# One encoder layer on one core: the residual rebuilt by TensorE, layer-norm scale and shift moved to evictions, first feed-forward pair's weight combinations kept

## The chip, the cores and the metric

The kernel runs on one core of a Trainium2 chip. The number that counts is the device time of one execution in microseconds (us), the median of several. The core's engines are PE (matrix multiply; PEld is its weight load), DVE (vector), ACT (scalar and activations), POOL (the third elementwise engine) and SP, which issues most of the DMA transfers. Each engine works through its own queue in order, so an instruction that waits holds up everything queued behind it on that engine.

## The reference

One layer, S = 1024 positions, D = 1024 channels, float32 in and out:

```
h = LN(x; ln0)
p = h @ w_in                        # 1024 -> 2048
y = [S5(p), RWKV-7(h, p), conv(p), Fourier(p)]
h = LN(alpha * h + y @ w_out; ln1)  # alpha = 2 ** 0.25
f = (silu(h @ w1) * (h @ w3)) @ w2  # 1024 -> 2816 -> 1024
out = LN(alpha * h + f; ln2)
```

LN subtracts the row mean, multiplies by the reciprocal deviation, then by a gain g and adds a shift b per channel. RWKV-7 is a scan over positions in two directions.

## The kernel before

Float32 products are made of three: each operand is split into a high part, cast to the type fp32r, and the low remainder, and `mm3` (L160 to L162) adds hi·hi, hi·lo and lo·hi in PSUM. `split_to` makes the parts: an ACT cast (L1384), then a subtraction on DVE or POOL (L1385).

**Order of the work.** `Trunk.build` weaves two generators with a list scheduler that sets each engine's queue order: `chain()` at high priority (S5, then the RWKV scan) and `beside()` (input projections, convolution, Fourier part, the second direction's preparation, output weights). The normalized input h lies transposed (channels on partitions) as `hhi` and `hlo` in the tiles HA0, HA1, HB0, HB1 until the last input projection; then these tiles take the data of the scan's other direction (HA0f to HB1f), which "inverse" and then the scan read.

**Output projection** (L1412 to L1500). For each tile t of 128 rows, from 7 down to 0: `residual` loads x and makes alpha·h again in row layout (L1432 DVE, L1434 POOL, L1435 DVE; the rows alpha·g, alpha·b, ln1_g, ln1_b come from `out_first`); `out_load` loads y and splits it (the subtraction on DVE for tiles 7 and 6, without a fixed engine for the rest); `out_product` runs 48 matmuls and adds PSUM to the residual (L1455); `norm` takes statistics and makes two passes (L1465, L1466). For each pair of tiles `turn` transposes on PE (L1518), copies out of PSUM on ACT (L1519), multiplies by alpha (L1520), stores to `d_acc`, and forms seven sums and differences of blocks, H[0] (first 512 positions, turns 0 and 1) or H[1] (turns 2 and 3).

**Feed-forward.** Products are made by a seven-multiplication scheme on 2 x 2 blocks. `ff_hidden` goes over 11 pairs p; each needs seven combinations of w1 and seven of w3, made by `ff_stream` (L1554 to L1583) in rings of tiles. Pair 0 runs as two halves of positions, `(0, (0,))` and `(0, (1,))`, so its first half can start before turns 2 and 3; the combinations are loaded and made once for each half. `put_by` splits and stores results to `d_f`. `ff_second` multiplies by w2: seven products n of 11 pairs, results added into `acc`; at n == 3 each of the eight `d_acc` tiles is loaded and added (L1783).

## Time and profile before

| what | value |
|---|---|
| median of 3 runs | 1462.27 us (1462.12 to 1463.15) |
| the profiled execution, own time | 1465.01 us |
| its span, first to last instruction | 1462.2 us |
| mean granted TensorE clock in it | 0.958 of full speed |
| PE, DVE, ACT, POOL busy | 90%, 75%, 43%, 39% |
| input projections; last matmul | to 454.8 us |
| output projection; last matmul | to 772.9 us |
| second stage of the feed-forward | 1228.8 to 1451.9 us |

How to read the rows below. A row of busy time gives the stretch, its length, then busy us of PE, PEld, DVE, ACT and POOL, each with its count of instructions in parentheses, then the granted TensorE clock, the DMA share and GB/s; "sum" adds all the tens of the query, also those not shown. A group of instructions has line, engine, operation, out<-in, shape and count, then busy us and mean ns of one, then the engine's idle time before it and what ended it. A wait has the total in us, how often, and the longest in us. A row on a tile's instructions has minimum, median and maximum ns, then the first and the last start.

### The profile page before, as it was taken

The numbers are of one execution on the slowest core, as the hardware profiler recorded it, in microseconds if no ns is written. First come the engines' busy times: TensorE is split into PE (matmuls) and PEld (weight loads), VectorE is DVE, ScalarE is ACT, GpSimd is POOL, SyncE is SP. The second block draws the span as 40 slices with busy tenths as digits, with TensorE's granted clock in tenths as the row PEclk, the third lists the DMA queues.
The fourth block names the chain that finished last, engine by engine and source line by source line (L and its number), as shares of the span: only waits on it lengthen the run. The fifth ranks groups of instructions, "written<-read, shape, count | busy, mean of one in ns | idle before, by whom it ended". The sixth has DMA issues, their size and how long they took to land.

```text
span 1462.2 us, 23749 instructions
## 1 busy us (share of the span) xinstructions
PE 1323.2 (90%) x9072; PEld 1196.4 (82%) x9072; DVE 1100.0 (75%) x1910; ACT 621.7 (43%) x1205; POOL 575.7 (39%) x524
## 2 busy tenths in 40 slices
PE   6968797977797999999877899999999999999997
...
GB/s 241 49 54 29 13 94 87 44 70 89 87 73 180 2 15 148 84 128 154 118 70 87 138 123 159 147 147 143 157 147 142 150 137 291 385 315 234 273 188 115
DMA packets 97056, 193.95 MB, mean 133 GB/s; under 512 B 24624, under 2 KB 50864, under 8 KB 96944
## 3 DMA queue, kind: packets, MB, share of 16 engines
...
## 4 chain that ended last, share of the span: by engine, by line
PE 42%; DVE 12%; DMA 3%; issue 2%; ACT 1%; POOL 1%; DVEq 0%; SPq 0%; ACTq 0%; POOLq 0%
PE fx L160 5%; PE fx L162 5%; PE fx L161 5%; PE f L160 4%; PE f L162 4%; PE f L161 4%; PE fy L162 2%; PE fy L160 2%; PE fy L161 2%; DVE acc L1435 1%; PE fz L160 1%; PE fz L161 1%; PE fz L162 1%; DMA fw<-w 1%; PE ops L161 1%
## 5 line engine op out<-in xcount | busy, mean ns | idle before, releaser
L160 PE MATMUL proj<-HA,wh 128*128 128x256 f32 x672 | 195.5, 291 | 14.6 <-DVE la L919 11.8
L160 PE MATMUL fx<-H,fc 128*128 128x256 f32 x704 | 196.9, 284 | 5.7 <-ACT fc L1384 2.2
L161 PE MATMUL proj<-HB,wh 128*128 128x256 f32 x672 | 200.1, 298 | 1.7 <-POOL HB L334 1.7
L162 PE MATMUL proj<-HA,wl 128*128 128x256 f32 x672 | 196.6, 293 | 4.1 <-POOL wl L394 4.1
L162 PE MATMUL fx<-H,fc 128*128 128x256 f32 x704 | 197.8, 282 | 2.6 <-DVE fc L1385 2.6
L1385 POOL TENSOR_TENSOR fc<-fw,fc 128x512 fp32r<-128x512 f32 x96 | 137.3, 1432 | 158.5 <-ACT fc L1384 157.7
L161 PE MATMUL fx<-H,fc 128*128 128x256 f32 x704 | 198.5, 282 | 0.0
L160 PEld LDWEIGHTS proj<-HA,wh 128*128 128x128 f32 x672 | 131.8, 196 | 18.4 <-issue 7.7
L162 PEld LDWEIGHTS proj<-HA,wl 128*128 128x128 f32 x672 | 131.5, 196 | 10.0 <-issue 5.5
L160 PEld LDWEIGHTS fx<-H,fc 128*128 128x128 f32 x704 | 132.5, 190 | 7.8 <-ACT fe L1633 2.7
L161 PEld LDWEIGHTS proj<-HB,wh 128*128 128x128 f32 x672 | 131.5, 196 | 7.0 <-issue 4.8
L162 PEld LDWEIGHTS fx<-H,fc 128*128 128x128 f32 x704 | 133.7, 191 | 2.8 <-DVE fc L1385 2.8
L161 PEld LDWEIGHTS fx<-H,fc 128*128 128x128 f32 x704 | 134.1, 191 | 0.1
L160 PE MATMUL f<-fb,fa 128*128 128x512 f32 x276 | 108.9, 395 | 0.0
L162 PE MATMUL f<-fb,fa 128*128 128x512 f32 x276 | 108.9, 394 | 0.0
L161 PE MATMUL f<-fb,fa 128*128 128x512 f32 x276 | 108.7, 394 | 0.0
L160 PE MATMUL fy<-H,fc 128*128 128x256 f32 x352 | 100.0, 284 | 4.7 <-ACT fe L1642 3.6
L162 PE MATMUL fy<-H,fc 128*128 128x256 f32 x352 | 99.5, 284 | 0.2 <-DVE fc L1385 0.2
L161 PE MATMUL fy<-H,fc 128*128 128x256 f32 x352 | 99.5, 283 | 0.0
L1821 POOL TENSOR_TENSOR acc<-acc,g 128x1024 f32<-128x1024 f32 x4 | 11.6, 2904 | 205.8 <-ACT acc L1820 205.8
L1384 ACT CAST fc<-fw 128x512 fp32r<-128x512 f32 x120 | 73.7, 619 | 31.8 <-POOL fc L1385 15.7
L1385 POOL TENSOR_TENSOR fc<-fs,fc 128x512 fp32r<-128x512 f32 x24 | 33.4, 1391 | 119.4 <-ACT fc L1384 116.0
...
## 6 DMA issues: line engine op xcount, KB each, us to landing
...
```

The source lines that it names most:

```text
L160: mm(out, whi, xhi, start=start, stop=False, skip_group_check=shared)
L161: mm(out, whi, xlo, start=False, stop=False, skip_group_check=shared)
L162: mm(out, wlo, xhi, start=False, stop=stop, skip_group_check=shared)
L1384: nc.scalar.copy(out=hi, in_=raw)
L1385: (eng or nc.gpsimd).tensor_tensor(out=lo, in0=raw, in1=hi.bitcast(F32), op=ALU.subtract)
L1435: nc.vector.tensor_tensor(out=ht, in0=ht, in1=self.row4[1], op=ALU.add)
L1821: nc.gpsimd.tensor_tensor(out=o, in0=o, in1=self.g2, op=ALU.mult)
```

## The change

1. `residuals()` turns h back to row layout on PE: 128 matmuls of 128x128 with `hhi` and `hlo` as stationary operand and an identity moving, in 16 groups of eight (one PSUM buffer of bank z), each group multiplied by alpha out of PSUM on ACT, and eight stores of 512 KB to `d_res`. It is woven with the convolution's projections. `residual` is now one load of `d_res`; its three passes, the four row loads and two ACT multiplications of `out_first` go.
2. `norm` is one DVE pass without g and b; `d_acc` is stored from there. `turn` applies g and b per channel while it leaves PSUM: four ACT activations of 128x128 in place of each copy of 128x512, and no multiplication by alpha. Turns 0 and 1 stand behind the output products of tiles 5 and 3.
3. `ff_second` makes up for it at n == 1 in place of n == 3: acc += alpha·b, x·(alpha·g) on POOL, acc += x.
4. In pair 0 the seven combinations of w1 are kept for both halves in a ring "k" (Z2, P2, P3, T7, WR, WH, WH); the order is w1 and w3 for half 0, then w1 and w3 for half 1, and results of pair 0 are put once at full width, 7 instead of 14.
5. `out_load` and `residual` of tile t - 1 are issued ahead of the product of tile t, and the split of y is always on DVE.

The diff, cut (the body of the loop in `ff_stream` moves into `parts` unchanged, and `ff_hidden` takes the steps of `ff_order`; `mm3` keeps its last matmul as `last_mm`, and `ff_second` loads the rows alpha·ln1_g and alpha·ln1_b first):

```diff
@@ -224,8 +225,10 @@
                     def beside():
-                        for part in (self.lora_project, self.rkv_project, self.conv, self.fourier_project):
+                        for part in (self.lora_project, self.rkv_project):
                             yield from part()
+                        yield from woven((self.conv(), 0), (self.residuals(), 0))
+                        yield from self.fourier_project()
...
@@ -268,6 +271,8 @@
+        self.ident_r = cp.tile([128, 128], R, name="ident_r")
+        nc.scalar.copy(out=self.ident_r, in_=self.ident)
@@ -1405,15 +1411,15 @@
+    def alpha_row(self, out, i):
+        self.row_load(out, i)
+        self.nc.scalar.mul(out=out, in_=out, mul=ALPHA)
-        rows = self.t("TT", [128, 4, D], "rows")
-        self.row4 = [rows[:, i] for i in range(4)]
-        for i in range(4):
-            self.row_load(rows[:, i], i)
-        for i in range(2):
-            nc.scalar.mul(out=rows[:, i], in_=rows[:, i], mul=ALPHA)
+        self.vec1 = self.cp.tile([128, 16], F32, name="vec1")
+        nc.scalar.dma_start(out=self.vec1, in_=self.A["vec1"])
@@ -1425,20 +1431,28 @@
         yield from self.out_product(7)
+    def residuals(self):
+        nc = self.nc
+        for t in range(NT - 1, -1, -1):
+            x = self.t(f"Z{t % 3}", [128, 2, 4, 128], "res")
+            for q in range(2):
+                ps = self.ps("z", [128, 4, 128], "rs")
+                for k in range(4):
+                    nc.tensor.matmul(ps[:, k, :], self.hhi[:, t, 4 * q + k, :], self.ident_r, start=True, stop=False)
+                    nc.tensor.matmul(ps[:, k, :], self.hlo[:, t, 4 * q + k, :], self.ident_r, start=False, stop=True)
+                nc.scalar.mul(out=x[:, q], in_=ps, mul=ALPHA)
+                yield 1.3
+            nc.sync.dma_start(out=self.d_res[t], in_=x.rearrange("p a k n -> p (a k n)"))
     def residual(self, t, tag):
-        nc = self.nc
-        ht = self.acc[t] = self.t(tag, [128, D], "acc")
-        nc.sync.dma_start(out=ht, in_=self.A["x"][t * 128:(t + 1) * 128, :])
-        nc.vector.tensor_scalar(out=ht, in0=ht, scalar1=self.st0[:, t, 0:1], scalar2=self.st0[:, t, 1:2],
-                                op0=ALU.subtract, op1=ALU.mult)
-        nc.gpsimd.tensor_tensor(out=ht, in0=ht, in1=self.row4[0], op=ALU.mult)
-        nc.vector.tensor_tensor(out=ht, in0=ht, in1=self.row4[1], op=ALU.add)
+        self.acc[t] = self.t(tag, [128, D], "acc")
+        self.nc.sync.dma_start(out=self.acc[t], in_=self.d_res[t])
     def out_load(self, t):
         nc = self.nc
         raw = self.raw("yraw").rearrange("p (k s) -> p k s", k=8)
         nc.sync.dma_start(out=raw, in_=self.d_y[:, :, t * 128:(t + 1) * 128].rearrange("k p s -> p k s"))
-        self.split_to(*self.y_parts(t), raw, nc.vector if t > 5 else None)
+        self.split_to(*self.y_parts(t), raw, nc.vector)
     def y_parts(self, t):
         return self.yp[t] if t < 7 else self.y7
@@ -1456,14 +1470,13 @@
     def out_proj(self):
         nc = self.nc
-        g1, b1 = self.row4[2:]
         self.raws = ["WR", "T7"]
         def norm(t):
             ht = self.acc[t]
             mean, rstd = self.row_stats(self.m, ht, D, LN_EPS)
-            nc.vector.scalar_tensor_tensor(out=ht, in0=ht, scalar=mean, in1=g1, op0=ALU.subtract, op1=ALU.mult)
-            nc.vector.scalar_tensor_tensor(out=ht, in0=ht, scalar=rstd, in1=b1, op0=ALU.mult, op1=ALU.add)
+            nc.vector.tensor_scalar(out=ht, in0=ht, scalar1=mean, scalar2=rstd, op0=ALU.subtract, op1=ALU.mult)
+            nc.sync.dma_start(out=self.d_acc[t], in_=ht)
         self.H = [[], []]
@@ -1478,14 +1491,16 @@
         self.out_load(6)
         self.residual(6, tag(6))
         for t in range(NT - 1, -1, -1):
-            if t < 7:
-                run(self.out_product(t))
             if 0 < t < 7:
                 self.out_load(t - 1)
                 self.residual(t - 1, tag(t - 1))
+            if t < 7:
+                run(self.out_product(t))
+            if t in (5, 3):
+                with self.tc.issue_after(self.last_mm.ins):
+                    self.turn(int(t == 3), [("P4", "P5", "Z0"), ("T6", "P0", "Z0")][t == 3])
             norm(t)
-            if t in (6, 4):
-                self.turn(3 - t // 2, [("P4", "P5", "Z0"), ("T6", "P0", "Z0")][t == 4])
             if t == 1:
                 self.combos = self.ff_stream()
                 self.ahead = [next(self.combos) for i in range(2)]
@@ -1516,9 +1531,11 @@
                 for k in range(4):
                     kt = 4 * q + k
                     nc.tensor.transpose(ps[:, k, :], ht[:, kt * 128:(kt + 1) * 128], self.ident)
-                nc.scalar.copy(out=dst[q], in_=ps)
-            nc.scalar.mul(out=ht, in_=ht, mul=ALPHA)
-            nc.sync.dma_start(out=self.d_acc[t], in_=ht)
+                for k in range(4):
+                    nc.scalar.activation(out=dst[q][:, k], in_=ps[:, k, :], func=AF.Identity,
+                                         scale=self.vec1[:, 4 * q + k:4 * q + k + 1],
+                                         bias=self.vec1[:, 8 + 4 * q + k:9 + 4 * q + k])
         H = self.H[j // 2]
         def put(i, x, eng):
@@ -1548,39 +1565,51 @@
     def ff_order(self):
-        return [(0, (0,)), (0, (1,))] + [(p, (0, 1)) for p in range(1, NF // 2)]
+        split = [(w, (h,)) for h in range(2) for w in range(2)]
+        return [split] + [[(w, (0, 1)) for w in range(2)] for p in range(1, NF // 2)]
     def ff_stream(self):
         nc, A = self.nc, self.A
         tt = nc.vector.tensor_tensor
-        self.rings = {"w": ["Z0", "Z1", "MW", "T6"], "s": ["P0", "P1"], "c": ["Z2", "P2", "LA0", "LA1", "C1", "C2"],
-                      "e": ["P3", "P4", "P5", "T5", "T7", "WR", "WL", "WL"], "g": ["WH", "WH"]}
+        self.rings = {"w": ["Z0", "Z1", "MW", "T6"], "s": ["P0", "P1"], "c": ["C1", "C2", "LA0", "LA1"],
+                      "e": ["P4", "P5", "T5", "WL", "WL"], "g": [], "k": ["Z2", "P2", "P3", "T7", "WR", "WH", "WH"]}
         self.banks = ["pj", "q", "fs", "q", "z", "pj", "q", "fs"]
         def split(x, eng=None):
-            c = self.ring("c", [128, 2, 4, 128], R)
+            c = self.ring(ring, [128, 2, 4, 128], R)
             self.split_to(c[:, 0], c[:, 1], x.rearrange("p (k n) -> p k n", k=4), eng)
             return c[:, 0], c[:, 1]
-        for p, hs in self.ff_order():
-            for nm in ("w1", "w3"):
...
+        def parts(nm, p):
...
+        for p, steps in enumerate(self.ff_order()):
+            kept = []
+            for w, hs in steps:
+                if kept and w == 0:
+                    yield from kept
+                    continue
+                ring = "c" if len(hs) == 2 or w else "k"
+                for x in parts(("w1", "w3")[w], p):
+                    if ring == "k":
+                        kept.append(x)
+                    yield x
     def ff_next(self):
         if len(self.ahead) < 4:
@@ -1643,22 +1672,27 @@
...
+        if p == 0:
+            k = self.rings["k"]
+            self.rings["c"] += k[:2]
+            self.rings["e"] += k[2:5]
+            self.rings["g"] += k[5:]
+    def put_by(self, m, p, x, y=None, op=None):
+        nc = self.nc
+        g = self.ring("g" if self.rings["g"] else "k", [128, 2, 512])
         if y is not None:
             nc.vector.tensor_tensor(out=g[:, 1], in0=x, in1=y, op=op)
             x = g[:, 1]
         self.split_to(g[:, 0].bitcast(R), g[:, 1], x, nc.vector)
-        nc.sync.dma_start(out=self.d_f[m, p, :, :, cs], in_=g)
+        nc.sync.dma_start(out=self.d_f[m, p], in_=g)
@@ -1776,11 +1811,15 @@
                     put(7 - 2 * j - s, h, sign, ps[j], n < 2)
                 if n == 5:
                     self.ff_out(7 - 2 * j)
-            if n == 3:
+            if n == 1:
                 for t in range(NT - 1, -1, -1):
                     x = self.ring("x", [128, D])
                     nc.sync.dma_start(out=x, in_=self.d_acc[t])
+                    tt(out=self.acc[t], in0=self.acc[t], in1=self.b2, op=ALU.add)
+                    nc.gpsimd.tensor_tensor(out=x, in0=x, in1=self.g2, op=ALU.mult)
                     tt(out=self.acc[t], in0=self.acc[t], in1=x, op=ALU.add)
+                self.row_load(self.g2, 4)
+                self.row_load(self.b2, 5)
         fill(la, ls, P)
         fill(ra, rs, P)
```

**Where instructions move.** PE among the input projections, near the end of `rwkv_first`: `pa` is a product of the scan's preparation, `proj` the input projections, `rs` the new groups. Before:

```order
L1132 MATMUL pa_4044<-abd_4001,bk_2860 128x128 x4
L160 MATMUL proj_3369<-HA_97,wh_3365 128x256
L161 MATMUL proj_3369<-HB_99,wh_3365 128x256
L162 MATMUL proj_3369<-HA_97,wl_3366 128x256
L160 MATMUL proj_3427<-HA_98,wh_3365 128x256
```

Now:

```order
L162 MATMUL proj_3507<-HB_103,wh_3447 128x256
L163 MATMUL proj_3507<-HA_101,wl_3448 128x256
L1138 MATMUL pa_4223<-abd_4180,bk_2863 128x128 x4
L1441 MATMUL rs_3301<-ident_r,HA_100 128x128
L1442 MATMUL rs_3301<-ident_r,HB_102 128x128
```

A group of eight `rs` matmuls (two shown) stands between a preparation product and the next projection; 12 of the 16 groups stand in this part of the queue, the first four earlier, among the S5 work.

POOL from the last part of the scan to the first turn: `TN` is the scan's gating, `y` and `H<-yraw` are splits of y, `H<-hb` splits of the turn. Before:

```order
L1434 TENSOR_TENSOR acc_6033<-acc_6033,rows_6026 128x1024
L1434 TENSOR_TENSOR acc_6554<-acc_6554,rows_6026 128x1024
L1434 TENSOR_TENSOR acc_6283<-acc_6283,rows_6026 128x1024
L1434 TENSOR_TENSOR acc_6357<-acc_6357,rows_6026 128x1024
L1376 TENSOR_TENSOR TN_6009<-TN_6009 128x256
L1385 TENSOR_TENSOR y_583_6278<-yraw_6353,y_582_6277 128x1024
L1434 TENSOR_TENSOR acc_6480<-acc_6480,rows_6026 128x1024
L1376 TENSOR_TENSOR TN_6139<-TN_6139 128x256
L1385 TENSOR_TENSOR H_6276<-yraw_6476,H_6276 128x1024
L1385 TENSOR_TENSOR H_6273<-hb_6376,H_6273 128x512
```

Now:

```order
L1382 TENSOR_TENSOR TN_5952<-TN_5952 128x256
L1382 TENSOR_TENSOR TN_6070<-TN_6070 128x256
L1382 TENSOR_TENSOR TN_6188<-TN_6188 128x256
L1382 TENSOR_TENSOR TN_6307<-TN_6307 128x256
L1382 TENSOR_TENSOR TN_6371<-TN_6371 128x256
L1391 TENSOR_TENSOR H_6444<-hb_6599,H_6444 128x512
L1382 TENSOR_TENSOR TN_6413<-TN_6413 128x256
L1391 TENSOR_TENSOR H_6446<-hb_6599,H_6446 128x512
L1391 TENSOR_TENSOR H_6445<-hb_6600,H_6445 128x512
```

Multiplications for the residual and splits of y are gone from this queue, and the turn's splits follow the gating directly.

POOL at the start of the first pair: `fc` and `fk` are combinations of w1 and w3 (`fk` those that are kept), `H<-hb` splits of turns 2 and 3. Before:

```order
L1385 TENSOR_TENSOR fc_6847<-fw_6843,fc_6847 128x512
L1385 TENSOR_TENSOR fc_6850<-fw_6843,fc_6850 128x512
L1385 TENSOR_TENSOR fc_7029<-fs_7023,fc_7029 128x512
L1385 TENSOR_TENSOR fc_7047<-fw_6844,fc_7047 128x512
L1385 TENSOR_TENSOR H_6918<-hb_6922,H_6918 128x512
L1385 TENSOR_TENSOR fc_7068<-fw_6844,fc_7068 128x512
L1385 TENSOR_TENSOR fc_7089<-fw_7085,fc_7089 128x512
L1385 TENSOR_TENSOR H_6918<-hb_6923,H_6918 128x512
L1385 TENSOR_TENSOR H_6919<-hb_6921,H_6919 128x512
L1385 TENSOR_TENSOR H_6918<-hb_6971,H_6918 128x512
```

Now:

```order
L1391 TENSOR_TENSOR fc_7273<-fw_7269,fc_7273 128x512
L1391 TENSOR_TENSOR H_7084<-hb_7088,H_7084 128x512
L1391 TENSOR_TENSOR fc_7345<-fw_7270,fc_7345 128x512
L1391 TENSOR_TENSOR H_7086<-hb_7088,H_7086 128x512
L1391 TENSOR_TENSOR H_7084<-hb_7089,H_7084 128x512
L1391 TENSOR_TENSOR H_7085<-hb_7087,H_7085 128x512
L1391 TENSOR_TENSOR H_7086<-hb_7088,H_7086 128x512
L1391 TENSOR_TENSOR H_7084<-hb_7145,H_7084 128x512
L1391 TENSOR_TENSOR fk_7213<-fs_7207,fk_7213 128x512
L1391 TENSOR_TENSOR fk_7231<-fw_7010,fk_7231 128x512
L1391 TENSOR_TENSOR fc_7380<-fw_7270,fc_7380 128x512
```

The third kept combination of w1 that POOL splits and the ones after it now stand behind six of turn 2's and 3's splits, and combinations of w3 stand ahead of them.

## Rows read from the trace of the kernel before

**Rows 1.** Page, parts 1 and 2: busy time, tenths in 40 slices.

```profile
PE 1323.2 (90%) x9072; PEld 1196.4 (82%) x9072; DVE 1100.0 (75%) x1910; ACT 621.7 (43%) x1205; POOL 575.7 (39%) x524
...
PE   6968797977797999999877899999999999999997
```

**Rows 2.** Busy time by tens, output projection and first pair.

```profile
740.00:750.00 10.00, 3.25 (x12) 2.36 (x11) 10.00 (x9) 3.69 (x6) 7.59 (x5) 0.76 0.08 18
...
800.00:810.00 10.00, 5.32 (x25) 4.34 (x23) 9.96 (x12) 6.69 (x15) 8.24 (x6) 0.66 0.00 0
...
sum 200.00, PE 170.98 PEld 147.14 DVE 184.67 ACT 80.32 POOL 117.54; mean PE 8.55 PEld 7.36 DVE 9.23 ACT 4.02 POOL 5.88
```

**Rows 3.** Waits of PE, 655 to 860 us.

```profile
PE ops L160 <- ACT H L1384: 6.7, 1, 6.7
...
PE pgn L1373 <- DVE TN L1374: 3.5, 2, 2.8
PE ops L160 <- DVE acc L1455: 3.1, 4, 1.4
PE ot L1518 <- DVE acc L1466: 2.7, 3, 1.8
```

**Rows 4.** Second stage: d_acc adds by line, busy time by tens.

```profile
L1783 DVE TENSOR_TENSOR acc<-acc,fx 128x1024 f32<-128x1024 f32 x8 | 9.7, 1219 | 3.7 <-DMA fx<-d_acc 3.7
...
sum 60.00, PE 60.00 PEld 48.52 DVE 28.15 ACT 17.96 POOL 0.00; mean PE 10.00 PEld 8.09 DVE 4.69 ACT 2.99 POOL 0.00
```

**Rows 5.** Busy time, a long stretch and tens, 310 to 410.

```profile
180.00:320.00 140.00, 123.70 (x866) 107.50 (x866) 89.82 (x88) 63.66 (x85) 58.72 (x56) 0.95 0.24 72
...
390.00:400.00 10.00, 5.48 (x39) 5.31 (x38) 9.27 (x11) 2.58 (x3) 3.07 (x3) 0.85 0.52 113
...
sum 100.00, PE 77.42 PEld 64.01 DVE 89.08 ACT 46.67 POOL 44.17; mean PE 7.74 PEld 6.40 DVE 8.91 ACT 4.67 POOL 4.42
```

**Rows 6.** Waits of PE, 320 to 470.

```profile
PE pa L1132 <- DVE abd L1129: 10.7, 3, 4.5
```

**Rows 7.** Tiles ot (690 to 694), proj and pz, instructions.

```profile
L1518 PE MATMUL ot<-ident,acc x8: 272/273/327, 692.3 to 693.2; 128*128 128x128 f32 x8
...
L162 PE MATMUL proj<-HA,wl x672: 274/280/687, 19.2 to 454.8; 128*128 128x256 f32 x168
...
L1297 PE MATMUL pz<-ring,HB1f x64: 272/275/377, 575.7 to 657.7; 128*128 128x128 f32 x64
```

**Rows 8.** Groups by line, 655 to 860: y splits, combinations.

```profile
L1575 DVE TENSOR_TENSOR fs<-fw 128x512 f32<-128x512 f32 x7 | 9.0, 1282 | 0.0
...
L1385 POOL TENSOR_TENSOR y<-yraw,y 128x1024 fp32r<-128x1024 f32 x3 | 7.7, 2568 | 1.3 <-ACT y L1384 1.3
...
L1432 DVE TENSOR_SCALAR acc<-acc,st 128x1024 f32<-128x1024 f32 x8 | 7.4, 920 | 2.1 <-DMA acc<-x 2.1
...
L1385 DVE TENSOR_TENSOR H<-yraw,H 128x1024 fp32r<-128x1024 f32 x1 | 1.2, 1226 | 0.0
```

**Rows 9.** Groups by line, residual and norm.

```profile
L1434 POOL TENSOR_TENSOR acc<-acc,rows 128x1024 f32<-128x1024 f32 x8 | 20.5, 2561 | 21.8 <-DVE acc L1432 14.3 <-DVE bnr L187 7.5
L1435 DVE TENSOR_TENSOR acc<-acc,rows 128x1024 f32<-128x1024 f32 x8 | 20.3, 2531 | 0.5 <-POOL acc L1434 0.5
...
L1466 DVE SCALAR_TENSOR_TENSOR acc<-acc,bnr,rows 128x1024 f32<-128x1024 f32 x8 | 16.0, 1995 | 0.2
...
L1465 DVE SCALAR_TENSOR_TENSOR acc<-acc,bnmv,rows 128x1024 f32<-128x1024 f32 x8 | 13.5, 1682 | 0.1
```

**Rows 10.** Groups by line: activation with scale, and the turn.

```profile
L332 ACT ACTIVATE hf<-n0ps,vec 128x128 f32<-128x128 f32 x40 | 14.7, 474 | 7.1 <-PE n0ps L322 5.1 <-POOL HB L334 2.0
...
L1519 ACT COPY hb<-ot 128x512 f32<-128x512 f32 x16 | 9.0, 584 | 12.3 <-PE ot L1518 7.1 <-DVE TN L1374 5.1
...
L1520 ACT ACTIVATE acc<-acc 128x1024 f32<-128x1024 f32 x8 | 8.5, 1066 | 0.0
```

102 lines of the change are left out of this document (51 added, 51 removed).

## The prediction

> **What bounds the kernel now.** First the page: PE is busy 90% of the span, DVE 75%, and the tenths of PE show 9 in nearly every slice from the 24th on and gaps before [rows 1]. So time can only be won where PE stands still, in the first two thirds. Then busy time in tens: from 660 to 860 us, the output projection and the start of the first feed-forward pair, PE works 170.98 of 200 us while DVE works 184.67. In the two worst tens PE works 3.25 and 5.32 us, DVE 10.00 and 9.96, and the granted clock falls to 0.76 and 0.66 [rows 2]. DVE sets the pace there, and 29.0 us of PE idle is all that can be won. Then the waits of PE: one of 6.7 us for the high and low part of a y tile, 3.5 us for the scan's gating, 3.1 us for the add that frees a PSUM bank, 2.7 us for a normalized tile before the turn [rows 3]; the other 13.0 us are small waits, mostly of the first pair. After that stretch PE is full (60.00 of 60 us in the second stage [rows 4]), so what is won by 860 us is kept to the end unless the second stage gets a stall.
>
> The early part pays. From 180 to 320 us PE works 123.70 of 140 us, from 310 to 410 us 77.42 of 100 while DVE works 89.08 [rows 5], and PE's waits there end on DVE (10.7 us for `pa` [rows 6]). The last projection starts at 454.8 us; only then can the tiles of h be given to the scan's second direction, whose first `pz` starts at 575.7 us [rows 7]. I take a delay of the last projection to be a delay of the scan and of everything behind it.
>
> **Residual.** Removed: L1432, 7.4 us of DVE [rows 8], L1434, 20.5 us of POOL, L1435, 20.3 us of DVE [rows 9]. L1435's mean is 2531 ns, the same shape as L1783 at 1219 ns [rows 4], where POOL is idle: it meets L1434 and the other POOL work of its stretch. The load stays (`d_res` for x). So DVE loses 27.7 us, POOL 20.5 us, and each tile's chain two engine changes.
>
> **Norm.** Two passes of 13.5 + 16.0 us [rows 9] become one. Nearest is L1432, a subtraction and a multiplication by two per-row scalars on 128x1024: 920 ns [rows 8], so 8 x 0.92 = 7.4 us, 22.1 us less on DVE.
>
> **Splits of y.** Six leave POOL (2568 ns, 15.4 us) and cost DVE 6 x 1.23 = 7.4 us [rows 8]. Since y and residual are issued a tile ahead of the product, the 6.7 us wait should go. On SP they are now queued ahead of the product's followers; the new store of `d_acc` waits on SP for `norm`, where before it waited for a later ACT instruction, so loads behind it do not come later than before.
>
> **Turn.** 64 activations with scale and shift at 474 ns, the price of L332, make 30.3 us; 9.0 us of copies and 8.5 us of multiplications go [rows 10]: ACT +12.8 us, to 93 of 200 [rows 2], no bound. But on the path of a turn the eviction of one tile takes 8 x 0.474 = 3.8 us where it took 2 x 0.584 = 1.2 us. For turns 0 and 1 output products cover this. For turns 2 and 3, the last thing before half 1, products of half 0 cover it; without that cover it is 2.6 us.
>
> **Kept combinations.** One of four sets of pair 0 is not made again: four DVE passes of 1282 ns (L1575 [rows 8], an upper price), about 5 us of DVE besides splits on three engines, and half the puts. It has its own price: the third kept combination that POOL splits waits there behind splits of turns 2 and 3. PE has the combinations of w3 for half 0 to work on meanwhile, so I cost it at nothing; uncovered, it shows as the rest of the idle time below.
>
> **What this stretch gives.** DVE: 184.7 - 27.7 - 22.1 + 7.4 - 5 = 137 of 200 us. POOL: 117.5 - 20.5 - 15.4 = 82. DVE no longer bounds it, PE does, with chains for the rest. Of the 29.0 us, 3.5 (the gating, untouched) stay; of the other 25.5 I leave 6 standing, about a quarter, for the last turns, the longer evictions and the first pair's own waits (a choice; between none and all, nearer none, since the engine that was full now has 30% of its time free). Gain 19.5 us, bounds 0 and 29.0.
>
> **Residual matmuls.** 128 of 128x128. In the nearest case, eight transposes of one turn start within 0.9 us [rows 7], 0.13 us each: 128 x 0.13 = 16.6 us. 12 of 16 groups stand in the part of the queue that ran from 310 to 410 us, where PE idles 22.6 us for DVE, the rest where it idles 16.3 of 140 [rows 5]. Work that stands before a waiting `pa` fills idle time, work behind it does not: I take half as hidden, 8 us of cost. Bounds: 0 (all hidden) and, with each group also holding PE for its eviction out of the one buffer of bank z (0.584 us, as L1519 [rows 10]), 16 x (1.04 + 0.58) = 26 us. ACT has room for the 16 evictions (46.67 of 100 [rows 5]); eight stores of 512 KB lie beside 100 us of work.
>
> **Second stage.** 16 DVE adds of 1219 ns, 19.5 us, where there were 8 later on; DVE works 28.15 of 60 us there and POOL nothing [rows 4], so 47.7 of 60: hidden, 0. POOL takes 8 x 2.56 = 20.5 us, as L1434. Queued behind an add that waits for its load and its multiplication are the splits of the next w2 products, for which PE waits; these are made ahead of time. Bounds 0 and 8.6, worked out under the third rival.
>
> **Sum.** 1465.0 (the profiled execution's own time, 2.8 us above its span) - 19.5 + 8 + 0 = 1453.5. The median of the runs shown lies 2.7 us below that execution, so I forecast **1451 us** for the median, 11.5 us less.
>
> **Rivals.** First: the whole gain, 25.5 us, with the early matmuls hidden: 1462.3 - 25.5 = 1437. For it: DVE, not PE, is full at 310 to 410 us [rows 5]. Against: the last tens before 454.8 us leave no room, and the two last turns wait on norm and ACT in any case.
>
> Second, slower: the early groups hold PE. Its queue is in order and the bank single: a group behind another waits until ACT has emptied it, and ACT's queue holds its own waiting work. At 1.62 us a group with nothing hidden, 26 us pass through the last projection and the scan to the end: 1462.3 - 19.5 + 26 = 1469. It decides from 19.5 / 16 = 1.2 us a group. Against: most groups are a dozen or more projection matmuls apart, time enough for an eviction.
>
> Third, no change: the second stage. L1435 beside POOL took 2531 ns where L1783 alone took 1219 [rows 4, 9]. The change puts 16 adds next to eight POOL multiplications. At 2.531 us they take 40.5 us; with 28.15 that is 68.6 of 60 us, DVE becomes the bound of products 1 and 2, and 8.6 us come back: 1460. Against: POOL is busy for only 20.5 us of it, and the adds of alpha·b need not meet it. The Trainium skill, "SBUF — State Buffer", section "Who interferes with whom", speaks for this rival: a DVE instruction with two SBUF inputs contends with a GpSimd (POOL) instruction that reads SBUF, whichever comes first holding the shared port while the other waits. By that rule every add that meets a multiplication waits for it, and the sum would be the third rival's, so far as they meet; L1435's 2531 ns against 1219 [rows 4, 9] agrees.
>
> That the change does not do what it says can be left out: the instructions stand in the order shown.
>
> **Chances.** A change within 0.2% (2.9 us) cannot be told from none. Forecast 0.58, all of its spread (19.5 give or take 6, 8 give or take 5) faster by more than that. Whole gain 0.17. Early groups hold PE 0.15, of which 0.03 ends within 0.2%. Second stage 0.10, mostly within. Faster 0.75, same 0.12, slower 0.13. The range goes from 1434 (all 29.0 us, nothing paid) to 1463; it leaves out most of the second rival.
>
> **What would show it.** Right: PE idle from the scan's last part to the first pair near 10 us instead of 29, DVE there near 137 us, the 6.7 us wait gone; `norm` near 0.92 us a tile; the last projection near 463 us and the first `pz` of the second direction near 584. Wrong: the last projection later than 470 us or waits of `rs` for ACT (second rival); DVE at 10 of 10 with PE waiting for splits of w2 products (third); or PE still waiting 20 us and more, for ACT's evictions of turns 2 and 3 or for kept combinations, which would mean that the cover I counted for them is not there.

## The result and the profile after

The change runs in 1439.56 us (median of 4, 1437.90 to 1440.89), the kernel before in 1462.19 us (median of 4, 1461.71 to 1463.15): ratio 0.9844, 95% interval 0.9827 to 0.9861. It is 22.6 us faster. The forecast was 1451 us, 11.5 us faster: the direction and the range held, the size was half of what came.

The page's busy line, PE's tenths and the granted clock in tenths, of the changed kernel, beside [rows 1]:

```profile
PE 1324.8 (92%) x9200; PEld 1203.7 (84%) x9200; DVE 1065.7 (74%) x1882; ACT 635.4 (44%) x1249; POOL 544.5 (38%) x513
...
PE   6968797978799998999998999999999999999997
...
PEclk9989898999799999999999999999999999999999
```

PE's busy time is 1324.8 us where it was 1323.2, though it runs 128 more matmuls. The span is 24.5 us shorter (1437.7 against 1462.2 us), and PE's tenths are 9 from the 17th slice on but for one 8 and the last, where before the gaps reached to the 23rd. (The profiled execution of before took 2.8 us more than its median, so spans differ by a little more than medians.)

Then the stretch that the prediction spoke of, 660 to 860 us, by busy time, beside the sum in [rows 2]:

```profile
660.00:860.00 200.00, 192.20 (x1244) 172.54 (x1243) 152.62 (x258) 97.23 (x212) 80.17 (x55) 0.99 0.40 132
```

PE works 192.20 us where it worked 170.98, DVE 152.62 instead of 184.67, POOL 80.17 instead of 117.54. PE's idle time fell from 29.0 to 7.8 us. Its longest waits there, in place of [rows 3]:

```profile
PE ot L1533 <- ACT hb L1536: 2.4, 2, 1.3
PE fx L161 <- ACT H L1390: 2.4, 1, 2.4
PE fx L162 <- POOL H L1391: 1.5, 1, 1.5
```

The waits of 6.7 us for y, of 3.5 us for the gating and of 3.1 us for the bank are gone. What is left first is the one that the prediction had named for the turns: eight small evictions instead of two, 2.4 us in all.

**Where the 24.5 us of the profile lie.** Three marks cut the span: the start of the last scan matmul (`pc`), the first matmul of the second stage (`f`), the end. Tile pc, instructions, before:

```profile
L1317 PE MATMUL pc<-ring,ring x256: 244/275/529, 489.8 to 676.3; 128*128 128x96 f32 x128
```

and after:

```profile
L1323 PE MATMUL pc<-ring,ring x256: 243/275/350, 498.1 to 683.4; 128*128 128x96 f32 x128
```

The scan ends at 683.4 instead of 676.3 us: 7.1 us are lost ahead of it. From there to the first `f` the kernel before takes 552.60 us; busy time of that stretch, before:

```profile
676.30:1228.90 552.60, 523.08 (x4014) 501.49 (x4013) 409.79 (x540) 250.17 (x459) 235.74 (x155) 0.98 0.41 137
```

The changed kernel takes 521.40 us, 31.2 less:

```profile
683.40:1204.80 521.40, 511.83 (x4002) 495.16 (x4001) 359.72 (x493) 251.39 (x483) 195.90 (x138) 1.00 0.42 143
```

Behind the first `f` 0.4 us are won (233.3 to 232.9 us). So −31.2 + 7.1 − 0.4 = −24.5. The middle term splits again. PE's idle time fell from 29.5 to 9.6 us, 19.9 us. Its **busy** time fell too, from 523.08 to 511.83 us, 11.25 us. The numbers of matmuls by tile (groups of that stretch) are alike: 2064 `fx`, 1032 `fy`, 528 `fz`, 64 `ot`, only 317 output products before and 306 after. The 11 that moved ahead of the scan's end start 0.23 us apart, 2.5 us. The other 8.7 us are the same matmuls in less time: the granted clock of the stretch is 0.98 before and 1.00 after. In the parts of it where the granted clock is 0.50, PE works 17.0 us before and 2.9 us after. A matmul there takes about twice as long (0.43 us against 0.23, below), so by this estimate some 7 of the 8.7 us are the clock. The rest is not assigned.

### The profile page after: what moved, and what is told of

It reads as the page before. It is cut to its first block, busy times and chain, and to the rows that moved or that the text cites. A ratio compares the mean times of both kernels' runs of the same rounds, so it can differ in the third digit from the quotient of the medians.

```text
span 1437.7 us, 23997 instructions
## 1 busy us (share of the span) xinstructions
PE 1324.8 (92%) x9200; PEld 1203.7 (84%) x9200; DVE 1065.7 (74%) x1882; ACT 635.4 (44%) x1249; POOL 544.5 (38%) x513
## 4 chain that ended last, share of the span: by engine, by line
PE 54%; DVE 27%; ACT 7%; DMA 5%; issue 4%; POOL 1%; SPq 1%; DVEq 0%; ACTq 0%; POOLq 0%
PE f L161 4%; PE fx L161 4%; PE f L163 4%; PE f L162 4%; PE fx L163 4%; PE fx L162 4%; PE ops L161 2%; PE ops L162 2%; PE ops L163 2%; PE fy L161 2%; PE fy L162 2%; PE fy L163 2%; DMA fw<-w 2%; PE proj L161 2%; PE proj L162 2%
## 5 line engine op out<-in xcount | busy, mean ns | idle before, releaser
L161 PE MATMUL proj<-HA,wh 128*128 128x256 f32 x672 | 201.9, 301 | 15.3 <-DVE la L925 11.1
L161 PE MATMUL fx<-H,fc 128*128 128x256 f32 x672 | 187.2, 283 | 2.5 <-ACT fe L1673 1.8
L162 PE MATMUL fx<-H,fc 128*128 128x256 f32 x672 | 189.5, 282 | 0.0
L163 PE MATMUL fx<-H,fc 128*128 128x256 f32 x672 | 189.0, 282 | 0.0
L1391 POOL TENSOR_TENSOR fc<-fw,fc 128x512 fp32r<-128x512 f32 x88 | 125.0, 1422 | 166.7 <-ACT fc L1390 165.8
L161 PEld LDWEIGHTS fx<-H,fc 128*128 128x128 f32 x672 | 126.5, 190 | 3.6 <-ACT fe L1673 2.6
L162 PEld LDWEIGHTS fx<-H,fc 128*128 128x128 f32 x672 | 127.6, 190 | 0.1
L163 PEld LDWEIGHTS fx<-H,fc 128*128 128x128 f32 x672 | 127.6, 190 | 0.0
L161 PE MATMUL fy<-H,fc 128*128 128x256 f32 x336 | 94.3, 281 | 0.4 <-ACT fe L1671 0.4
L162 PE MATMUL fy<-H,fc 128*128 128x256 f32 x336 | 94.3, 281 | 0.0
L163 PE MATMUL fy<-H,fc 128*128 128x256 f32 x336 | 94.2, 280 | 0.0
L1390 ACT CAST fc<-fw 128x512 fp32r<-128x512 f32 x110 | 67.8, 621 | 32.3 <-POOL fc L1391 14.3
L1391 POOL TENSOR_TENSOR fc<-fs,fc 128x512 fp32r<-128x512 f32 x22 | 30.1, 1369 | 105.9 <-ACT fc L1390 104.6
L1390 ACT CAST fb<-fs 128x512 fp32r<-128x512 f32 x47 | 29.1, 623 | 92.3 <-PE f L163 59.7
```

The lines of the kernel that those rows point to most:

```text
L161: mm(out, whi, xhi, start=start, stop=False, skip_group_check=shared)
L162: mm(out, whi, xlo, start=False, stop=False, skip_group_check=shared)
L163: self.last_mm = mm(out, wlo, xhi, start=False, stop=stop, skip_group_check=shared)
L1390: nc.scalar.copy(out=hi, in_=raw)
L1391: (eng or nc.gpsimd).tensor_tensor(out=lo, in0=raw, in1=hi.bitcast(F32), op=ALU.subtract)
```

## The experiments

The change ran in a set of its own, the other kernels in four sets on four chips. Each set holds runs of the kernel before, so ratios are compared, not times, and a difference of two ratios has the uncertainty of both.

| kernel | median us | ratio to before, 95% interval |
|---|---|---|
| the change | 1439.56 | 0.9844, 0.9827 to 0.9861 |
| part 1 (residual) undone | 1453.65 | 0.9935, 0.9917 to 0.9954 |
| parts 2 and 3 (norm, second stage) undone | 1442.49 | 0.9869, 0.9844 to 0.9894 |
| part 4 (kept combinations) undone | 1449.34 | 0.9909, 0.9889 to 0.9928 |
| part 5 (a tile ahead) undone | 1438.63 | 0.9832, 0.9811 to 0.9853 |
| before with part 1 alone | 1462.54 | 0.9995, 0.9977 to 1.0013 |
| half the early matmuls (low parts of h left out) | 1431.95 | 0.9784, 0.9762 to 0.9807 |
| twice the early matmuls | 1457.66 | 0.9965, 0.9952 to 0.9978 |
| before with 24 filler matmuls | 1470.45 | 1.0049, 1.0033 to 1.0065 |
| part 1 undone, 128 unread matmuls early | 1458.99 | 0.9958, 0.9943 to 0.9972 |
| residual early on DVE, among the S5 work | 1469.76 | 1.0035, 1.0023 to 1.0047 |
| residual early on DVE, behind the last S5 convolution steps | 1427.52 | 0.9761, 0.9746 to 0.9775 |
| residual early on DVE, behind the last S5 output | 1445.85 | 0.9885, 0.9868 to 0.9901 |

### One part undone at a time

Four kernels, each the changed one with a part put back. Part 1 undone:

```diff
-                        yield from woven((self.conv(), 0), (self.residuals(), 0))
+                        yield from self.conv()
...
-        self.nc.sync.dma_start(out=self.acc[t], in_=self.d_res[t])
+        nc.sync.dma_start(out=ht, in_=self.A["x"][t * 128:(t + 1) * 128, :])
+        nc.vector.tensor_scalar(out=ht, in0=ht, scalar1=self.st0[:, t, 0:1], scalar2=self.st0[:, t, 1:2],
+                                op0=ALU.subtract, op1=ALU.mult)
+        nc.gpsimd.tensor_tensor(out=ht, in0=ht, in1=self.row4[0], op=ALU.mult)
+        nc.vector.tensor_tensor(out=ht, in0=ht, in1=self.row4[1], op=ALU.add)
```

> The changed kernel with part 1 undone: the residual is again made from x by DVE, POOL and DVE, no matmuls among the projections. Theory (DVE sets the pace of the output projection, the early matmuls cost 7 us up to the scan's end): the early 7 us come back, and about half of the 31 us behind the scan is lost, since 27.7 of the 49 us taken off DVE return: 1439.6 - 7 + 15 = 1448 us, PE idle behind the scan 20 us or more against 10. Rival (DVE has slack once any one part has gone, and the early matmuls were pure cost): 1432 us, PE idle unchanged.

Parts 2 and 3 undone (the turns keep their new place behind the products):

```diff
-            nc.vector.tensor_scalar(out=ht, in0=ht, scalar1=mean, scalar2=rstd, op0=ALU.subtract, op1=ALU.mult)
-            nc.sync.dma_start(out=self.d_acc[t], in_=ht)
+            nc.vector.scalar_tensor_tensor(out=ht, in0=ht, scalar=mean, in1=g1, op0=ALU.subtract, op1=ALU.mult)
+            nc.vector.scalar_tensor_tensor(out=ht, in0=ht, scalar=rstd, in1=b1, op0=ALU.mult, op1=ALU.add)
...
+                nc.scalar.copy(out=dst[q], in_=ps)
+            nc.scalar.mul(out=ht, in_=ht, mul=ALPHA)
+            nc.sync.dma_start(out=self.d_acc[t], in_=ht)
...
-            if n == 1:
+            if n == 3:
```

> The changed kernel with parts 2 and 3 undone: norm in two passes with gain and shift, plain copies in the turn, alpha on ACT, the d_acc tiles added at n == 3. Theory (DVE sets the pace): 22 of the 49 us return to DVE, 5 to 12 us are lost: 1445 to 1452 us. Rival (the longer evictions of turns 2 and 3 cost as much as the pass saves): 1439 us or less, the wait of fx for splits of H shorter.

Part 4 undone (with the rings, the puts and the loop as before):

```diff
-        split = [(w, (h,)) for h in range(2) for w in range(2)]
-        return [split] + [[(w, (0, 1)) for w in range(2)] for p in range(1, NF // 2)]
+        return [(0, (0,)), (0, (1,))] + [(p, (0, 1)) for p in range(1, NF // 2)]
```

> The changed kernel with part 4 undone: the combinations of w1 for pair 0 are made twice again. Theory (5 us of DVE and two loads less, covered): 1 to 4 us slower, 1441 to 1444 us. Rival (the kept combinations are what fills PE between 770 and 860 us, where 14.7 us of idle time fell to 7): 8 us or more slower, 1448 us.

Part 5 undone:

```diff
-        self.split_to(*self.y_parts(t), raw, nc.vector)
+        self.split_to(*self.y_parts(t), raw, nc.vector if t > 5 else None)
...
+            if t < 7:
+                run(self.out_product(t))
             if 0 < t < 7:
                 self.out_load(t - 1)
                 self.residual(t - 1, tag(t - 1))
-            if t < 7:
-                run(self.out_product(t))
```

> The changed kernel with part 5 undone: y and the residual are loaded behind the product of the tile before, and y of tiles 5 to 0 is split without a fixed engine. Theory (the 6.7 us wait for y comes back, and matmuls behind a wait run at the lower clock): 6 to 10 us slower, 1446 to 1450 us. Rival (with POOL free of the residual the split comes in time anyway): within 2 us of 1439.6.

Taken out of the change, the residual costs (0.9935 − 0.9844) x 1462 = 13 us, the kept combinations 9.5 us, the norm 3.7 us and a tile ahead −1.8 us; the last two are within the intervals. The residual cost more than expected, the kept combinations and the tile ahead came out as their rivals had it, and for the norm the runs do not decide. The waits say where the two large ones come from. Without part 1, PE's waits for the add out of PSUM and for the norm return (waits of PE from the scan's end to the first `f`):

```profile
PE ops L161 <- DVE acc L1479: 7.8, 2, 4.3
PE ot L1543 <- DVE acc L1488: 6.5, 2, 4.5
```

Without part 4, PE waits in the first pair for splits of combinations (waits of PE from the first `fx` to the first `f`):

```profile
PE fx L163 <- DVE fc L1391: 5.6, 1, 5.6
PE fx L163 <- POOL fc L1391: 4.0, 4, 1.6
```

Neither group is among the waits of the change in that stretch. In part 4's case the stretch from the scan's end holds exactly the same matmuls as in the change, 2064 `fx`, 1032 `fy`, 528 `fz`, 306 output products:

```profile
681.20:1213.50 532.30, 517.31 (x4002) 499.72 (x4001) 370.56 (x511) 256.31 (x497) 203.91 (x143) 0.99 0.41 142
```

It takes 10.9 us more than the 521.40 us of the change: 5.4 us of idle time (15.0 against 9.6) and 5.5 us of busy time (517.31 against 511.83), at a granted clock of 0.99 instead of 1.00; where the granted clock is 0.50, PE works 12.4 us instead of 2.9. Here an idle microsecond is paid about twice. From before to the change it is paid 1.4 times (28.6 us for 19.9).

Part 5 undone leaves PE even a little fuller from 660 to 860 us (193.29 us busy). The wait for y that it was to remove is not there without it either, nor in the kernel with part 1 alone (below). The likely reason is that DVE and POOL have less to do ahead of the split; this was not tested by itself.

### The residual alone, and the price of the early matmuls

The kernel before with part 1 alone, `residuals` and `residual` as in the change:

```diff
-                        for part in (self.lora_project, self.rkv_project, self.conv, self.fourier_project):
+                        for part in (self.lora_project, self.rkv_project):
                             yield from part()
+                        yield from woven((self.conv(), 0), (self.residuals(), 0))
+                        yield from self.fourier_project()
```

> The kernel before with part 1 alone: residual by matmuls and one load, everything else as it was. Theory (the residual's three passes held the scan's last gating and the products, some 20 us behind the scan; the matmuls cost 7 to 9 us ahead of it): 1462 - 21 + 8 = 1449 us, the last pgn as early as in the changed kernel (705) or earlier. Rival (it pays only together with the shorter norm, since DVE stays full with two-pass norms): the 8 us remain, 1462 to 1470 us.

The change with half the early matmuls (the residual is then that of the high parts of h alone, so this is a measurement and not a version to use):

```diff
-                    nc.tensor.matmul(ps[:, k, :], self.hhi[:, t, 4 * q + k, :], self.ident_r, start=True, stop=False)
-                    nc.tensor.matmul(ps[:, k, :], self.hlo[:, t, 4 * q + k, :], self.ident_r, start=False, stop=True)
+                    nc.tensor.matmul(ps[:, k, :], self.hhi[:, t, 4 * q + k, :], self.ident_r, start=True, stop=True)
```

> The changed kernel with half the early matmuls: the low parts are left out, so the residual is that of the high part alone. Theory (half of the matmul time hides, as the prediction said): 64 matmuls less are 8.3 us of PE, 4 us come back, 1435.5 us, the last projection 4 us or more earlier. Rival (the early cost is the moved order of the projections, not the matmuls): within 2 us of 1439.6.

With twice as many:

```diff
-                    nc.tensor.matmul(ps[:, k, :], self.hhi[:, t, 4 * q + k, :], self.ident_r, start=True, stop=False)
-                    nc.tensor.matmul(ps[:, k, :], self.hlo[:, t, 4 * q + k, :], self.ident_r, start=False, stop=True)
+                    for again in range(2):
+                        nc.tensor.matmul(ps[:, k, :], self.hhi[:, t, 4 * q + k, :], self.ident_r, start=True, stop=False)
+                        nc.tensor.matmul(ps[:, k, :], self.hlo[:, t, 4 * q + k, :], self.ident_r, start=False, stop=True)
```

> The changed kernel with each early matmul group run twice over, the same result: 256 matmuls. Theory (half hides): 16.6 us of PE more, 8 us slower, 1447.5 us; at most 16.6 if the idle time is used up. Rival (order, not matmuls): within 2 us of 1439.6.

Part 1 undone, and `residuals` put on top of that kernel for its matmuls alone:

```diff
-                nc.scalar.mul(out=x[:, q], in_=ps, mul=ALPHA)
-            nc.sync.dma_start(out=self.d_res[t], in_=x.rearrange("p a k n -> p (a k n)"))
```

> The changed kernel with part 1 undone (u_res, 1453.7 us, residual by DVE and POOL behind the scan), but with the 128 early matmuls kept in their place; their results are not read, and neither evicted nor stored. Theory A (the full price of PE time): 1453.7 + 16.6 = 1470 us. Theory B (half of it is hidden or won back, because PE, kept busy past 455 us, runs the scan at the higher clock: lost clock between 470 and 660 us about 12 us without early matmuls and 4 us with 128 of them): about 1462 us, the scan's last pc 7 to 9 us later than in u_res, its lost clock near 4 us.

**The residual alone is worth nothing** (0.9995), as the rival of its expectation had it. From the scan's end to the first `f` of that kernel:

```profile
676.20:1226.30 550.10, 529.49 (x4034) 508.15 (x4033) 395.31 (x527) 249.99 (x458) 222.78 (x149) 0.98 0.41 140
```

20.6 us of idle time stay, where the change leaves 9.6. PE's longest waits in it:

```profile
PE fx L160 <- ACT fe L1650: 4.2, 2, 2.8
PE ops L160 <- DVE acc L1466: 4.0, 2, 3.6
PE fx L162 <- DVE fc L1390: 3.1, 1, 3.1
PE fy L162 <- POOL fc L1390: 2.2, 1, 2.2
```

The waits for split combinations (`fc`, 3.1 and 2.2 us) are of the kind that part 4 removes, and the wait for the bank is still there; the wait for y is not. Behind the scan's end the part does win something alone: from 552.6 us with 317 output products to 550.1 with 336 it is 6.9 us, at 0.23 us a product. Of these, 4.3 us are paid ahead of the scan's end (the table below). Put last, from part 1 undone (544.0 us with 321 products) to the change (521.4 with 306), it wins 19 us there. Undone one at a time the four parts are worth some 25 us, and the one that is worth most, 13 us, is worth nothing alone. The idle time fits this account: the parts take work off the same DVE, and with part 1 alone PE waits for its other work.

**The price of the early matmuls** is read at the scan's end, with the output products that stand ahead of it taken out (306 to 336 of them lie behind it; 0.23 us each, brought to 317 as before):

| early matmuls | kernel | scan's last `pc` us | output products behind | at 317 us |
|---|---|---|---|---|
| 0 | before | 676.3 | 317 | 676.3 |
| 0 | part 1 undone | 674.6 | 321 | 675.5 |
| 64 | half | 671.3 | 332 | 674.8 |
| 128 | the change | 683.4 | 306 | 680.9 |
| 128 | part 1 alone | 676.2 | 336 | 680.6 |
| 128 | unread ones | 675.2 | 336 | 679.6 |
| 256 | twice | 695.4 | 332 | 698.9 |

By these rows the first 64 cost nothing, 128 cost 4 to 5 us, the next 128 cost 18 us, 0.14 us each, which is the whole price that the prediction took (0.13). That leaves room for some 90 to 100 of them. It is an estimate: there is one profile of each kernel, so a microsecond or two may be chance, and it assumes that a product ahead of the scan's end delays it by its full 0.23 us. Whole times put the room lower: half is 0.9784 against 0.9844, 8.8 us less than the change for 64 matmuls, which is their whole price (64 x 0.14 = 9.0), so there is room for little more than 64. Twice is 17.7 us more for 128. Both are about twice what the expectations had (4 and 8 us). The unread matmuls cost at the scan's end what the read ones cost (679.6 beside 680.6 and 680.9 us), and 3.4 us in whole time (0.9958 against 0.9935), less than either theory had; so it is PE's time that is paid, not the evictions or the stores.

### Does a matmul in the wait keep the clock?

The kernel before has a wait of 6.75 us in tile 1's product [rows 3]. PE's instructions around it, in order of time (start, us, idle time before and what ended it):

```profile
741.51 0.39 PE L162 MATMUL ops<-owb,H 128*128 128x512 f32 x1
748.65 0.77 PE L160 MATMUL ops<-owa,y 128*128 128x512 f32 x1 [6.75 <-ACT H L1384]
749.21 0.63 PE L161 MATMUL ops<-owa,y 128*128 128x512 f32 x1
749.64 0.63 PE L162 MATMUL ops<-owa,y 128*128 128x512 f32 x1
750.07 0.63 PE L160 MATMUL ops<-owa,y 128*128 128x512 f32 x1
...
752.36 0.39 PE L160 MATMUL ops<-owc,y 128*128 128x512 f32 x1
```

Ahead of the wait matmuls start 0.23 us apart. Behind the second one after it, six start 0.43 us apart, later ones 0.23 to 0.24 again. The granted clock is 0.50 from 748.7 to 751.7 us: the engine stood still, came back at the lower of the clock's two levels (1.2 GHz) and rose to 2.4 GHz. To test whether an engine that works through the wait keeps its clock, 24 matmuls that read only weights were put ahead of that product:

```diff
+            if t == 1 and n == 0:
+                for i in range(24):
+                    self.nc.tensor.matmul(ps, self.wo8[0][0][:, :128], self.wo8[0][0][:, :512], start=True, stop=True)
```

> The kernel before with 24 matmuls that nobody reads (the product of tile 1 overwrites them) ahead of the product that waits 6.7 us, so that PE works through that wait. Theory (matmuls behind a stall run at the lower granted clock, and this was the part of the gain that the sum left out): the granted clock between 740 and 760 us stays at 1.00, the matmuls behind the wait start every 0.23 us instead of 0.43, some 2 us are won, 1460 us. Rival (the slow matmuls come from something else, such as the memory that they read): clock and pitch as before, 1462 us.

It missed: the fillers did not run during the wait. PE's instructions in order of time:

```profile
745.98 2.50 PE L1453 MATMUL ops<-owa 128*128 128x512 f32 x5 [6.76 <-DVE acc L1458]
...
753.19 0.39 PE L160 MATMUL ops<-owa,y 128*128 128x512 f32 x1
753.42 0.39 PE L161 MATMUL ops<-owa,y 128*128 128x512 f32 x1
```

and busy time by stretches:

```profile
742.00:750.00 8.00, 4.02 (x10) 3.19 (x11) 7.93 (x12) 3.74 (x6) 6.88 (x4) 0.57 0.39 126
750.00:758.00 8.00, 8.00 (x36) 6.57 (x35) 8.00 (x9) 0.19 (x1) 4.97 (x3) 1.00 0.02 7
```

The filler itself waited 6.76 us, for the DVE add that empties its PSUM bank. In the kernel before, the same add starts at 747.82 us and takes 0.68, so the bank came free only just ahead of the product. So the wait on record as one for y had two conditions, and the other was hidden behind it. The kernel became 7 us slower (1.0049). It shows one thing: the slow start goes with the wait, not with the data. The fillers took 753.19 − 745.98 = 7.2 us, 0.30 each, at a granted clock of 0.57 in their stretch, and the products of y behind them started at once at 0.23. Whether a filler that could run during the wait would hold the clock was not tried.

**Idle time and busy time side by side.** All rows run from the scan's end to the first `f`; 2064 `fx`, 1032 `fy`, 528 `fz` and 64 `ot` are in each, and output products over 306 are taken off at 0.23 us. Part 1 undone:

```profile
674.60:1218.60 544.00, 523.07 (x4017) 502.91 (x4017) 384.10 (x522) 251.64 (x485) 213.00 (x144) 0.98 0.39 137
```

Parts 2 and 3 undone:

```profile
674.00:1207.70 533.70, 521.41 (x4034) 502.15 (x4034) 381.52 (x515) 245.10 (x444) 203.75 (x139) 0.99 0.41 142
```

Part 5 undone:

```profile
684.10:1204.40 520.30, 512.92 (x4003) 496.40 (x4003) 357.85 (x487) 251.03 (x483) 207.99 (x143) 0.99 0.41 143
```

| kernel | output products | PE idle us | busy us | busy, at 306 |
|---|---|---|---|---|
| part 5 undone | 306 | 7.4 | 512.9 | 512.9 |
| the change | 306 | 9.6 | 511.8 | 511.8 |
| parts 2 and 3 undone | 336 | 12.3 | 521.4 | 514.5 |
| part 4 undone | 306 | 15.0 | 517.3 | 517.3 |
| part 1 alone | 336 | 20.6 | 529.5 | 522.6 |
| part 1 undone | 321 | 20.9 | 523.1 | 519.6 |
| before | 317 | 29.5 | 523.1 | 520.6 |

With 7 to 10 us of idle time the same matmuls take 512 to 513 us; with 20 us and more they take 520 to 523 (among these three the order is not that of the idle time).

### The residual early, on DVE

If PE's time ahead of the scan's end is full, the residual could be made early elsewhere. Three kernels take `residuals()` of the change, but make alpha·h out of x by two DVE passes of 128x1024 a tile; the second and the third differ only in where the 16 passes stand in DVE's queue. The first stands among the S5 work, and for that it is woven with other projections, so its difference from the other two is not the place alone:

```diff
-                        for part in (self.lora_project, self.rkv_project):
-                            yield from part()
-                        yield from woven((self.conv(), 0), (self.residuals(), 0))
+                        yield from self.lora_project()
+                        yield from woven((self.rkv_project(), 0), (self.residuals(), 0))
+                        yield from self.conv()
...
-                    nc.tensor.matmul(ps[:, k, :], self.hhi[:, t, 4 * q + k, :], self.ident_r, start=True, stop=False)
...
+            nc.vector.scalar_tensor_tensor(out=x, in0=x, scalar=self.st0[:, t, 0:1], in1=g, op0=ALU.subtract, op1=ALU.mult)
+            nc.vector.scalar_tensor_tensor(out=x, in0=x, scalar=self.st0[:, t, 1:2], in1=b, op0=ALU.mult, op1=ALU.add)
```

> The changed kernel with the residual made early without PE: x is loaded again beside the projections, DVE makes alpha times the normalized row with gain and shift in two passes and stores it to d_res; no early matmuls. Theory (the changed kernel has no slack left on PE, so that 64 matmuls less gave 7.6 us and 128 more cost 18: the full price each way; DVE is idle a third of 180 to 320 us): the 128 matmuls come back whole, 1439.6 - 16.6 = 1423 us, up to 1430 if the two passes of 1.3 us hold up the preparation of the scan. Rival (DVE sets the pace of the early stage too): 16 passes, 21 us, come on top: 1440 us or more.

The second and third queue the same two lines behind a chosen instruction (`self.mark`): the second behind the last steps of the S5 convolution, the third behind the last S5 output.

```diff
+            self.mark = tt(out=vi[q], in0=vi[q], in1=m0, op=ALU.add)
...
+            with self.tc.issue_after(self.mark.ins):
```

> As v_rkv (residual made early by DVE, no early matmuls), but the 16 passes are queued behind the last S5 convolution steps, where DVE idles most (some 32 us between 240 and 300 us), instead of ahead of them. Theory (v_rkv lost 38 us because its passes stood among S5 work on a full DVE; behind the scan it kept the gain): the scan starts as early as without matmuls or up to 10 us later, 1423 to 1435 us. Rival (any 21 us of DVE ahead of the scan is paid in full): 1439.6 - 16.6 + 21 = 1444 us.

> As v_m1, with the passes queued a little later, behind the last S5 output, so that more of them stand among the preparation of the scan, where DVE is nearly full. Theory (the place on DVE decides): 3 to 10 us slower than v_m1. Rival (price of DVE time alone): the same as v_m1 within 2 us.

The first pass of each tile, instructions of tile res: shortest, median and longest ns, first and last start. Among the S5 work:

```profile
L1442 DVE SCALAR_TENSOR_TENSOR res<-res,st,resrow x8: 1268/1284/2104, 65.4 to 187.1; 128x1024 f32<-128x1024 f32 x8
```

Behind the convolution steps:

```profile
L1443 DVE SCALAR_TENSOR_TENSOR res<-res,st,resrow x8: 1258/1286/3369, 245.5 to 321.7; 128x1024 f32<-128x1024 f32 x8
```

Behind the last S5 output:

```profile
L1443 DVE SCALAR_TENSOR_TENSOR res<-res,st,resrow x8: 1273/1281/1284, 257.8 to 352.5; 128x1024 f32<-128x1024 f32 x8
```

The same 16 passes of about 1.28 us give 1.0035, 0.9761 and 0.9885: 40 us between the first place and the second, and 18 us between the second and the third, which differ in nothing else. The second came out as its theory had it; the first was expected at 1423 to 1430 us, and the third 3 to 10 us behind the second. In the first place, from 65 us on, they stand among the passes of S5 and of the low-rank projections, and a projection of PE waits for one of the latter (L937; waits of PE, 180 to 480 us):

```profile
PE proj L161 <- DVE lg L937: 15.9, 1, 15.9
```

and the scan ends at 714.7 us. Behind the last S5 output they last until 359 us and stand among the preparation of the scan, whose product `pa` waits 14.4 us:

```profile
PE pa L1138 <- DVE abd L1135: 14.4, 5, 5.8
```

In the second place they start at 245 us and are done by 330 us, and the same wait is 5.8 us:

```profile
PE pa L1138 <- DVE abd L1135: 5.8, 3, 2.4
```

There the scan ends at 663.9 us, and the stretch behind it costs what it costs in the change, with 26 more output products in it:

```profile
663.90:1191.80 527.90, 518.05 (x4031) 500.57 (x4031) 361.75 (x504) 251.43 (x484) 196.42 (x139) 0.99 0.42 144
```

**This second version, 1427.52 us (0.9761, 0.9746 to 0.9775), beats both kernels**, the change by 12 us. Why its scan ends 8 us earlier than with no early residual at all (667.4 against 675.5 us, both at 317 output products) is open. PE's waits for DVE at `pa` and at `pre` (L1138 and L1092) are shorter in it (5.8 and 5.0 us, against 10.6 and 10.0 with part 1 undone; waits of PE, 0 to 480 us), but the weaving also moved the convolution's projections, and that was not tried by itself.

## Why the prediction saw half of the gain

**The sum.** It had −19.5 for idle time, +8 for the early matmuls, 0 for the second stage. Measured: −19.9 us of idle time, +4.6 us (7.1 at the scan's end less 2.5 for the 11 moved products), −0.4 us. These three give −15.7. The other −8.7 us, slower matmuls that are gone, had no term. In the profiles the gain is 24.5 us, 13 us more than forecast: 8.7 are this term, 3.4 the early matmuls, which were priced too high, and 0.4 each the other two.

**The step that failed** is "29.0 us of PE idle is all that can be won". It took PE's busy time as a floor. The prediction quoted the granted clocks of 0.76 and 0.66 in the two worst tens [rows 2] and put no price on them. In the profile of before, the 523.08 us of busy time behind the scan hold 17.0 us at a granted clock of 0.50; the change has 2.9 there, and its busy time for the same matmuls is 8.7 us less. So even the bound "all 29.0 us, nothing paid" was none. The Trainium skill, "TensorE: Matmul & The Clock Gate", Part 1, has the two levels and says that an engine that has been idle runs at the lower one. The trace agrees, with 0.43 us a matmul after the 6.75 us wait and 0.23 ahead of it.

**The early matmuls.** "I take half as hidden" was near by the scan's end (4.6 of 16.6 us paid; taking half of them away gave 8.8 us back in whole time). Its reason was not: a delay of the last projection is not a delay of the scan. Tiles proj and pz in the change, beside [rows 7]:

```profile
L163 PE MATMUL proj<-HA,wl x672: 274/281/1202, 19.3 to 483.8; 128*128 128x256 f32 x168
```

```profile
L1303 PE MATMUL pz<-ring,HB1f x64: 275/275/377, 588.5 to 667.7; 128*128 128x128 f32 x64
```

The last projection starts 29.0 us later (483.8), the first `pz` of the second direction 12.8 us later, the scan ends 7.1 us later. By the prediction's own mark, "later than 470 us", the second rival should have come. It did not: the late projections fill PE where it had stood idle. Busy time from 470 to 560 us, before:

```profile
470.00:560.00 90.00, 78.86 (x545) 67.72 (x543) 67.02 (x192) 65.20 (x182) 29.88 (x77) 0.89 0.07 21
```

and after, with 116 more matmuls on record and a granted clock of 0.98 instead of 0.89:

```profile
470.00:560.00 90.00, 84.60 (x661) 74.95 (x659) 63.20 (x191) 63.59 (x193) 32.82 (x84) 0.98 0.11 38
```

**The parts.** 19.5 us was right as a sum and wrong in its shares, so that the sum came so close is partly luck. Credit for the 6.7 us wait went to part 5, whose removal costs nothing that the runs can tell; the wait is gone with part 1 alone. Kept combinations, of which the prediction counted 5 us of DVE time, are worth 9.5 us, about half in idle time and half in slower matmuls. Their own price, "cost at nothing", held: from the scan's end to the first `f` no wait of PE in the change is for `fk`.

**Prices.** Norm and eviction by group, beside [rows 8, 10]:

```profile
L1536 ACT ACTIVATE hb<-ot,vec 128x128 f32<-128x128 f32 x64 | 23.9, 488 | 6.7 <-issue 3.5 <-PE ot L1533 3.2
...
L1478 DVE TENSOR_SCALAR acc<-acc,bnmv,bnr 128x1024 f32<-128x1024 f32 x8 | 7.1, 884 | 0.3
```

0.884 us a tile (0.92 expected) and 0.488 (0.474). DVE from 660 to 860 us came to 152.62 us, not 137; part of it is that the first pair starts 15 us earlier, so more of it lies in the stretch.

**The rivals.** The first (1437) is the nearest in number, but not by its mechanism: 9.6 us of idle time stayed, and the matmuls were not free. The second fell: `rs` waits for ACT 1.9 us in all. The third fell as a time, but DVE and POOL did hold each other up, only in other instructions than it had named. Instructions of tile acc in the change, the 16 adds of the second stage:

```profile
L1818 DVE TENSOR_TENSOR acc<-acc,rmask x8: 1217/1217/1224, 1243.2 to 1280.1; 128x1024 f32<-128x1024 f32 x8
L1820 DVE TENSOR_TENSOR acc<-acc,fx x8: 1212/1216/1219, 1256.5 to 1326.0; 128x1024 f32<-128x1024 f32 x8
```

No add took more than 1224 ns, where L1435 of before reached 3448 (instructions of that line):

```profile
L1435 DVE TENSOR_TENSOR acc<-acc,rows x8: 1210/2976/3448, 667.7 to 748.4; 128x1024 f32<-128x1024 f32 x8
```

The adds hardly meet the eight multiplications, which wait one by one for loads of `d_acc`. Splits and sums of the w2 products do meet them: beside each multiplication one DVE pass of 128x512 takes 2.4 to 2.9 us, where others take 0.7. Two of POOL's, in order of time:

```profile
1265.33 2.44 POOL L1819 TENSOR_TENSOR fx<-fx,g 128x1024 f32<-128x1024 f32 x1 [10.29 <-DMA fx<-d_acc]
1283.48 4.87 POOL L1819 TENSOR_TENSOR fx<-fx,g 128x1024 f32<-128x1024 f32 x1 [15.72 <-DMA fx<-d_acc]
```

The second is twice as long as the first. DVE beside it and beside the next one, which starts at 1288.52 (x2 is two passes):

```profile
1283.00 1.29 DVE L1763 TENSOR_TENSOR fs<-fg,fg 128x512 f32<-128x512 f32 x2
1284.20 1.29 DVE L1391 TENSOR_TENSOR fb<-fs,fb 128x512 fp32r<-128x512 f32 x2
...
1286.44 2.46 DVE L1391 TENSOR_TENSOR fb<-fs,fb 128x512 fp32r<-128x512 f32 x1 [0.35 <-ACT fb L1390]
1288.82 2.89 DVE L1763 TENSOR_TENSOR fs<-fg,fg 128x512 f32<-128x512 f32 x1
```

As long as DVE's passes follow one another (to 1286.1 us) they keep their 0.6 to 0.7 us, and the multiplication is the one that is drawn out; the pass that DVE starts after a pause of 0.35 us takes 2.46 us. The Trainium skill, "SBUF — State Buffer", "Who interferes with whom", says that the order of issue, not the shape of the operation, decides which of the two engines blocks. These rows agree as far as they go: both outcomes stand in one multiplication of 4.87 us. PE never waits for it: it is busy 60.00 of the 60 us from 1270 to 1330. DVE had the room, though less than counted, 54.84 us where 47.7 were expected (beside [rows 4]; sum of the tens from 1270 to 1330 us):

```profile
sum 60.00, PE 60.00 PEld 48.61 DVE 54.84 ACT 16.84 POOL 16.08; mean PE 10.00 PEld 8.10 DVE 9.14 ACT 2.81 POOL 2.68
```

Only 11 of the 16 adds stand in these 60 us, but five of the long passes do, some 10 us more than their kind takes. The second stage as a whole is 0.4 us shorter than before, so the term of 0 was right; but the count of DVE's time behind it had left the held-up passes out, and 5 us of room were left where 12 were counted.
